# SSD decays in tiles of their own, two buffers for ec, and a HGRN norm one head earlier, in pieces

## The chip, the cores and the metric

The kernel runs on one core of one Trainium2 chip. The metric is the device time of one execution in microseconds (us). TensorE is called PE (its weight loads PEld), VectorE DVE, ScalarE ACT, GpSimd POOL and SyncE SP. Each engine works through its own queue in order; a semaphore wait holds up everything behind it on that engine.

## The reference

One inference step of two layers, each followed by a SwiGLU FFN: a Mamba-2 SSD layer and an HGRN2 layer, model width 1024, for 1024 frames of a new stream and 32 frames of a running one. The work is split in two halves of 512 and 544 columns. The scans are chunked; in the reference the SSD step is

```python
cum = jnp.cumsum(dtc * Ag, axis=1)
seg = cum[:, :, None] - cum[:, None, :]
decay = jnp.where(mask, jnp.exp(jnp.where(mask, seg, 0.0)), 0.0)
cb = jnp.einsum('btgn,bsgn->btsg', Cc, Bc)
y = jnp.einsum('btsg,btsgh,bsghp->btghp', cb, decay, xdt)
y = y + jnp.einsum('btgn,bghpn->btghp', Cc, S) * jnp.exp(cum)[..., None]
S = jnp.exp(last)[..., None, None] * S + jnp.einsum('bsgh,bsghp,bsgn->bghpn', w_end, xdt, Bc)
```

The decays of a chunk are exponentials of clamped differences of running sums; y multiplies them by C times B, and by x times dt. The HGRN layer has a gated linear recurrence per head. Each layer begins with an RMS norm: y = x * rsqrt(mean(x * x) + eps) * w.

## The kernel before, in words

Activations stand with features on the partitions and time along the row. Every large product is made of three matmuls (L314, L315, L316): the weight is split into a rounded part wh (ACT copies it, L98) and a rest wl (DVE subtracts, L101), the activation likewise (xn; h and l). A raw weight block is loaded by SP (helper `dma`, L110); three raw buffers and three pairs of wh and wl rotate. Helpers record most instructions: ACT has L98, DVE L101 (two tensors) and L104 (scalar, tensor, tensor).

The SSD layer has eight units, two halves by four groups of eight heads. A unit's work list holds the output product of the unit before (`ssd_out`), its own four z products (`ssd_z`), and late in the unit the convolutions of the next one. Its chunks of 128 columns (four in half one; four and one of 32 in half two) are spread over this list. A scheduler then places the instructions; parts marked `lifted` get a priority (`HP`, L112): a norm 600, a gate 100, a chunk 0.

A chunk (`ssd_chunk`, from L543) does this. `chunk_loads` has SP load the running sums of 2 times 4 heads, broadcast over the partitions, into two cumB tiles (tag "cb", four buffers), and the decays of the incoming state into an ec tile (tag "ec", one buffer). PE multiplies C with B (L552), DVE masks that (cbm). PE transposes x (L557), DVE makes xdt and xw from it. For each cumB tile ACT runs four Relus (each head's difference of running sums, clamped, in place), one Exp over the tile, and DVE multiplies by cbm (L570), in place too. PE transposes B (L572) and ACT copies it to Btok ("fixed<-sc 128x128"). L579 multiplies the state with C, L582 makes the new state part from Btok and xw, and L593 multiplies xdt with the decays in cumB. DVE then adds the ec part to give Y. `ssd_z` evacuates the z product on ACT (Tanh) and DVE (z<-z,mm). At the end of a unit `ssd_gate` squares Y on ACT, adds the squares on DVE, and L331 sums them over partitions for the norm (`rstd_of`, L318: squares, L331, Ln, Exp; ACT loads a table ahead of Ln and of Exp).

The HGRN layer has 16 units, two halves by eight heads (e = 0 to 7), each with chunks of which L806 to L825 are the PE part; hkv, hg, ho and hy are tiles of a head. The products of the next head (f, q, v) and the output of each two finished heads (L314 to L316 on hy) fill PE between. Half two's norm must stand before head (1, 0)'s products, which are in the work of head (0, 7). It is made with priority 600 by `norm` in the work list of head (0, 6): eight squares, the sum L331, Ln, Exp, and then for each of eight blocks of features a product on DVE (xf), a copy on ACT (h) and a subtraction on DVE (l). The results go into twelve "x" and four "cb" buffers.

Of the kernel before, what the change touches and what calls it, by code (L numbers as in the profile page):

```python
# [11 lines left out]
AF = mybir.ActivationFunctionType  # L12
# [4 lines left out]
P = 128  # L17
# [5 lines left out]
LEN = (H1, SEQ - H1 + NS)  # L23
# [14 lines left out]
C_SSDN, C_CB, C_FFN, C_HGN, C_GN, C_HG, C_LB = 0, 8, 32, 48, 56, 72, 73  # L38
# [2 lines left out]

TW = 552
FIXED = 14368
BUFS = {"x": 12, "ys": 8, "cb": 4, "xd": 2, "ec": 1, "ss": 1, "xr": 2, "n": 4, "w": 3}
WIDTH = {k: TW for k in BUFS}


@with_exitstack
def trunk_kernel(ctx, tc, x_prompt, x_sample, state_ssd, cache_conv, state_hgrn,
# [16 lines left out]
    def nm(s):  # L66
        uid[0] += 1
        return f"{s}_{uid[0]}"

    def T(tag, s, dt=F32):  # L70
        return tp.tile([P, WIDTH[tag]], dt, tag=tag, bufs=BUFS[tag], name=nm(s))

    def slot(tag, s):
        return T(tag, s, F32R) if isinstance(tag, str) else tag
# [22 lines left out]
    def act(out, in_, f, **kw):  # L97
        A.activation(out=out, in_=in_, func=f, **kw)  # L98
# [58 lines left out]
    for i in range(2):  # L157
        t = place(P)
# [8 lines left out]
    xr = place(9)  # L167
# [170 lines left out]
    XN = [xnt[:, i] for i in range(16)]  # L338
    XN2 = ["x"] * 12 + ["cb"] * 4
# [39 lines left out]
    @lifted("norm")  # L379
    def norm(h, wc, out, tags, blocks=None, r=None):  # L380

        for (b0, bn) in blocks or ((0, LEN[h]),):
            mmb = BLK[h] if blocks is None else [(0, bn)]
            if r is None:
                r = rstd_of([acc[h][m][:, b0:b0 + bn] for m in range(KD)], mmb, 1.0 / D, bn)
            for m in range(KD):
                xf = T("n", "xf")
                stt(xf[:, :bn], acc[h][m][:, b0:b0 + bn], vc[:, wc + m:wc + m + 1], r[:, :bn], MUL, MUL)
                if m == len(out):
                    out.append((slot(tags[2 * m], "h"), slot(tags[2 * m + 1], "l")))  # L390
                xh, xl = out[m]
                act(xh[:, b0:b0 + bn], xf[:, :bn], AF.Copy)
                tt(xl[:, b0:b0 + bn], xf[:, :bn], xh[:, b0:b0 + bn].bitcast(F32), SUB)
        return out
# [8 lines left out]
    st = [place(TW) for _ in range(NG)]  # L403
# [138 lines left out]
    @lifted("chunk")  # L542
    def ssd_chunk(h, g, c, S, loads, u):  # L543
        o, n, smp = CHUNKS[h][c]
        Bt, Ct, xs, Y = u["x"][0], u["x"][1], u["x"][2:], u["Y"]
        cols, elast = dts[h]
        xo = o + (3 if smp else 0)
        Bx, Cx = Bt[:, xo:xo + n], Ct[:, xo:xo + n]
        h0 = g * 8
        cums, ec = loads  # L550
        ps = psum_sc()
        PE.matmul(ps[:n, :n], Bx, Cx, start=True, stop=True)  # L552
        cbm = small("cbm")
        tt(cbm[:n, :n], ps[:n, :n], cmask[:n, :n], MUL)
        ps = psum_sc()
        for j in range(4):
            PE.transpose(ps[:n, j * P:(j + 1) * P], xs[j][:, xo:xo + n], ident)  # L557
        x3 = ps[:n, :].rearrange("p (h q) -> p h q", q=64)
        xdt, xw = T("xd", "xdt")[:, :512], T("xd", "xw")[:, :512]
        tt(xdt[:n, :].rearrange("p (h q) -> p h q", q=64), x3,  # L560
           cols[:n, c, h0:h0 + 8].unsqueeze(2).to_broadcast([n, 8, 64]), MUL)
        tt(xw[:n, :].rearrange("p (h q) -> p h q", q=64), x3,
           cols[:n, c, 64 + h0:64 + h0 + 8].unsqueeze(2).to_broadcast([n, 8, 64]), MUL)
        for q in range(2):
            cb3 = cums[q]
            for i in range(4):
                hh = 32 + h0 + 4 * q + i
                act(cb3[:n, i, :n], cb3[:n, i, :n], AF.Relu, scale=-1.0, bias=cols[:n, c, hh:hh + 1])
            act(cb3[:n, :, :n], cb3[:n, :, :n], AF.Exp, scale=-1.0)
            tt(cb3[:n, :, :n], cb3[:n, :, :n], cbm[:n, :n].unsqueeze(1).to_broadcast([n, 4, n]), MUL)  # L570
        ps = psum_sc()
        PE.transpose(ps[:n, :P], Bx, ident)  # L572
        Btok = small("Btok")
        act(Btok[:n, :], ps[:n, :P], AF.Copy)
        if ec is not None:
            y2 = psum_sc()
            y23 = y2.rearrange("p (j t) -> p j t", t=P)
            for j in range(4):
                PE.matmul(y23[:, j, :n], S[:, j * P:(j + 1) * P], Cx, start=True, stop=True)  # L579
            tt(ec[:, :, :n], y23[:, :, :n], ec[:, :, :n], MUL)  # L580
        pp = psum_sc()
        PE.matmul(pp, Btok[:n, :], xw[:n, :], start=True, stop=True)  # L582
        if ec is None:
            V.tensor_copy(S, pp)
        else:
            S3 = S.rearrange("p (h q) -> p h q", q=64)
            tt(S3, S3, elast[:, h0:h0 + 8, c:c + 1].to_broadcast([P, 8, 64]), MUL)
            tt(S, S, pp, ADD)
        y1 = psum_sc()
        y13 = y1.rearrange("p (j t) -> p j t", t=P)  # L590
        for i in range(8):
            r = 64 * (i % 2)
            PE.matmul(y13[r:r + 64, i // 2, :n], xdt[:n, i * 64:(i + 1) * 64], cums[i // 4][:n, i % 4, :n],  # L593
                      start=True, stop=True)
        yo = Y[:, :, o:o + n]
        if ec is None:
            act(yo, y13[:, :, :n], AF.Copy)
        else:
            tt(yo, y13[:, :, :n], ec[:, :, :n], ADD)
# [260 lines left out]
    def hgrn_layer(after):  # L860
        units = [(h, e) for h in range(2) for e in range(8)]
        us = [{"S": None} for _ in units]
        for f in (hgrn_f, hgrn_q, hgrn_v):
            f(0, 0, us[0])
        for i, (h, e) in enumerate(units):
            u = us[i]
            tasks = [lambda: hgrn_g(h, e, u)]
            if e % 2 == 0 and i:
                ph, pe = units[i - 1]
                tasks += [lambda m4=m4: hgrn_out(ph, pe // 2, m4, [us[i - 2]["y"], us[i - 1]["y"]])  # L870
                          for m4 in range(2)]
            if i + 1 < len(units):
                nh, ne = units[i + 1]
                tasks += [lambda f=f: f(nh, ne, us[i + 1]) for f in (hgrn_f, hgrn_q, hgrn_v)]
            if (h, e) == (0, 6):
                tasks.append(lambda: norm(1, C_HGN, xns[1], XN2))
            if (h, e) == (1, 6):
                tasks += after[:1]
            if (h, e) == (1, 7):
                tasks += after[1:]  # L880
            u["o"] = T("ys", "ho")
            if e % 2 == 0:
                yt = sp.tile([P, 4 * TW], F32R, tag="Y", bufs=1, name=nm("hy"))[:, :4 * LEN[1]]
                yp = yt.rearrange("p (j t) -> p j t", j=4)
            u["yp"] = yp
            nch = len(CHUNKS[h])
            for c in range(nch):
                second = hgrn_chunk(h, e, c, u)
                q = -(-len(tasks) // (nch - c))
                for i2, t in enumerate(tasks[:q]):  # L890
                    if i2 == HB2:
                        second()
                    t()
                if q <= HB2:
                    second()
                tasks = tasks[q:]
            hgrn_gate(h, e, u)
        return [lambda m4=m4: hgrn_out(1, 3, m4, [us[-2]["y"], us[-1]["y"]]) for m4 in range(2)]
# [6 lines left out]
    def x_stat(h, keep):  # L905

        return rstd_of([acc[h][m][:, :LEN[h]] for m in range(KD)], BLK[h], 1.0 / D, LEN[h], keep)

    def norm_pieces(h, wc, out, blocks, r):

        def piece(m, b0, bn):
            xf = T("n", "xf")
            stt(xf[:, :bn], acc[h][m][:, b0:b0 + bn], vc[:, wc + m:wc + m + 1], r[:, b0:b0 + bn], MUL, MUL)
            if m == len(out):
                out.append((XN[2 * m], XN[2 * m + 1]))
            xh, xl = out[m]
            act(xh[:, b0:b0 + bn], xf[:, :bn], AF.Copy)
            tt(xl[:, b0:b0 + bn], xf[:, :bn], xh[:, b0:b0 + bn].bitcast(F32), SUB)
        return [lambda m=m, b=b: piece(m, *b) for b in blocks for m in range(KD)]
# [209 lines left out]
    def mixed(a, b):  # L1129

        out, k = [], 0
        for i, x in enumerate(a):
            out.append(x)
            while k < len(b) and k * len(a) < (i + 1) * len(b):
                out.append(b[k])
                k += 1
        return out + b[k:]
# [98 lines left out]
    xns, dts = [[], []], [None, None]  # L1236
# [12 lines left out]
    due, r = mixer_ffn(lambda after: ssd_layer(after, w0), 0, C_FFN, True)  # L1249
# [9 lines left out]
    due, r = mixer_ffn(hgrn_layer, 1, C_FFN + 8, False)  # L1259
# [41 lines left out]
```

## Time and profile before

| | |
|---|---|
| median of three runs | 2903.72 us (2901.35 to 2903.73) |
| profiled execution, device time | 2906.18 us |
| profiled execution, span | 2904.4 us |
| mean granted clock of PE | 0.996 |
| PE busy | 2848.8 us, 98% |
| DVE busy | 2152.7 us, 74% |
| ACT busy | 1559.5 us, 54% |
| SSD layer's chunks, first to last L593 | 97.6 to 856.8 us |
| half one's first 128x512 stall of L582 in unit 1 | 187.58 us |
| the HGRN norm of half two, PE's waits | 1838 to 1846 us |

In the quoted rows a timeline gives the start, the duration, the engine, the line, the operation, output<-inputs by the program's names without buffer numbers, the shape, how many in a row, and in brackets the idle time just before with what ended it. A row of waits gives the waiting engine and line, what it waited for, the sum in us, how often, and the longest. A row of a stretch gives the start and end, its length, then the busy time (and number of instructions) of PE, PEld, DVE, ACT and POOL, then the clock that PE was granted (PEclk, 1.00 is full speed), the share of the DMA engines and GB/s.

### The profile page before, as it was taken

Reading aid. Unit: us, or ns where it says so; the run is one execution under the profiler, and the core shown is the slowest. Engines: PE = TensorE matmul, PEld = TensorE weight load, DVE = VectorE, ACT = ScalarE, POOL = GpSimd, SP = SyncE. Lnnn points to the kernel's source line nnn. Section 1 sums busy time; section 2 is a strip of 40 time slices with the busy share of each in tenths; the row PEclk is TensorE's granted clock in tenths of the full one; section 3 lists DMA queues with packets and bytes.
Section 4 is the critical chain, followed back from the end, with each engine's and each line's share of the span. In section 5 each row is a group of like instructions: output and inputs, shape, how many; then the busy total and the mean of one; then the engine's idle time right before and its main releaser. Section 6 shows DMA issues by size and latency. Waiting matters only on the chain. (4 is left out here: it accounts for less than half of the span.)

```text
span 2904.4 us, 49072 instructions
## 1 busy us (share of the span) xinstructions
PE 2848.8 (98%) x19711; PEld 2619.9 (90%) x19711; DVE 2152.7 (74%) x3744; ACT 1559.5 (54%) x2922; POOL 46.4 (2%) x156
## 2 busy tenths in 40 slices
PE   8999999999999999999999999999999999999998
PEld 7777788999988999999999888899988999999998
DVE  6777787777787977887777455655568877887777
ACT  6645645554653754456544655655554644554445
POOL 0000000000000000000000000000000000000000
PEclk9999999999999999999999999999999999999999
DMA  5443434344332333323333222222222332333223
GB/s 151 115 111 92 110 82 120 109 114 108 107 90 88 102 111 100 102 80 95 109 95 105 81 82 73 60 79 77 74 84 81 119 100 88 120 94 94 90 88 111
DMA packets 401247, 282.61 MB, mean 97 GB/s; under 512 B 22633, under 2 KB 388730, under 8 KB 401018
## 3 DMA queue, kind: packets, MB, share of 16 engines
q1 hardware_dynamic: 401018, 279.47, 33.2%
q8 instruction: 154, 2.52, 0.3%
q14 instruction: 75, 0.61, 0.1%
HBM read 271.61 MB, written 7.82 MB: 96 GB/s over the span
## 5 line engine op out<-in xcount | busy, mean ns | idle before, releaser
L98 ACT ACTIVATE wh<-raw 128x512 fp32r<-128x512 f32 (+1 forms) x688 | 557.3, 818 | 541.8 <-PE mm L315 419.5
L314 PE MATMUL mm<-xn,wh 128*128 128x272 f32 (+2 forms) x1552 | 524.8, 338 | 0.3 <-ACT wh L98 0.3
L315 PE MATMUL mm<-xn,wh 128*128 128x272 f32 (+2 forms) x1552 | 519.1, 335 | 3.8 <-issue 3.8
L316 PE MATMUL mm<-xn,wl 128*128 128x272 f32 (+2 forms) x1552 | 518.5, 334 | 3.2 <-DVE wl L101 3.2
L101 DVE TENSOR_TENSOR wl<-raw,wh 128x1024 fp32r<-128x1024 f32 x308 | 375.9, 1222 | 83.7 <-ACT wh L98 63.5
L101 DVE TENSOR_TENSOR fixed<-mm,fixed 128x272 f32<-128x272 f32 (+1 forms) x512 | 262.9, 525 | 192.7 <-PE mm L316 191.1
L314 PE MATMUL mm<-fh,wh 128*128 128x272 f32 (+1 forms) x1056 | 341.7, 325 | 1.1 <-DVE fixed L101 0.8
L315 PE MATMUL mm<-fl,wh 128*128 128x272 f32 (+1 forms) x1056 | 341.9, 324 | 0.7 <-DVE fl L101 0.7
L316 PE MATMUL mm<-fh,wl 128*128 128x272 f32 (+1 forms) x1056 | 341.7, 324 | 0.0
L316 PEld LDWEIGHTS mm<-xn,wl 128*128 128x128 f32 x1552 | 293.0, 189 | 37.3 <-issue 6.0
L314 PEld LDWEIGHTS mm<-xn,wh 128*128 128x128 f32 x1552 | 293.0, 189 | 29.5 <-issue 2.6
L315 PEld LDWEIGHTS mm<-xn,wh 128*128 128x128 f32 x1552 | 293.0, 189 | 27.1 <-issue 0.8
L101 DVE TENSOR_TENSOR wh<-raw,wh 128x512 fp32r<-128x512 f32 x380 | 257.1, 688 | 38.5 <-ACT wh L98 35.2
L989 PE MATMUL mm<-th,wh 128*128 128x272 f32 (+1 forms) x912 | 260.4, 286 | 0.1
L990 PE MATMUL mm<-tl,wh 128*128 128x272 f32 (+1 forms) x912 | 259.7, 285 | 0.0
L991 PE MATMUL mm<-th,wh 128*128 128x272 f32 (+1 forms) x912 | 259.6, 285 | 0.0
L314 PEld LDWEIGHTS mm<-fh,wh 128*128 128x128 f32 x1056 | 198.4, 188 | 17.4 <-DVE fixed L101 1.7
L315 PEld LDWEIGHTS mm<-fl,wh 128*128 128x128 f32 x1056 | 198.7, 188 | 16.3 <-DVE fl L101 1.8
L316 PEld LDWEIGHTS mm<-fh,wl 128*128 128x128 f32 x1056 | 198.7, 188 | 15.3
L989 PE MATMUL sc<-xn,wh 128*128 128x272 f32 (+1 forms) x608 | 173.2, 285 | 0.5 <-ACT wh L98 0.5
L989 PEld LDWEIGHTS mm<-th,wh 128*128 128x128 f32 x912 | 171.8, 188 | 1.9 <-ACT s L98 1.2
L990 PE MATMUL sc<-xn,wh 128*128 128x272 f32 (+1 forms) x608 | 173.2, 285 | 0.0
(251 smaller groups left out, 6637.0 us busy)
## 6 DMA issues: line engine op xcount, KB each, us to landing
raw<-in_ffn_w_down_dram SPq DMA_DIRECT2D x90, 512.0 KB, 3.5
raw<-in_ffn_w_gate_dram SPq DMA_DIRECT2D x88, 512.0 KB, 3.8
raw<-in_ffn_w_up_dram SPq DMA_DIRECT2D x88, 512.0 KB, 4.6
raw<-in_ssd_in_w_dram SPq DMA_DIRECT2D x80, 512.0 KB, 4.0
raw<-in_hgrn_in_w_dram SPq DMA_DIRECT2D x64, 512.0 KB, 4.2
cumB<-cumd SPq DMA_DIRECT2D x64, 256.0 KB, 4.5
raw<-in_ssd_out_w_dram SPq DMA_DIRECT2D x32, 512.0 KB, 3.5
raw<-in_hgrn_out_w_dram SPq DMA_DIRECT2D x16, 512.0 KB, 3.3
```

The source lines that it names most:

```text
L98: A.activation(out=out, in_=in_, func=f, **kw)
L101: (eng or V).tensor_tensor(out=out, in0=a, in1=b, op=op)
L314: PE.matmul(ps[:, :bn], a, mh, start=(k == 0), stop=False)
L315: PE.matmul(ps[:, :bn], a, ml, start=False, stop=False)
L316: PE.matmul(ps[:, :bn], b, mh, start=False, stop=(k == n - 1))
L989: PE.matmul(ps[:, :n], a, mh, start=(k == 0 and not more), stop=False, skip_group_check=True)
L990: PE.matmul(ps[:, :n], a, ml, start=False, stop=False, skip_group_check=True)
L991: PE.matmul(ps[:, :n], b, mh, start=False, stop=(k == 3), skip_group_check=True)
```

## The change

Three things. The Relus of a chunk read cumB as before but write to a new tile "dec" (tag "de", two buffers); Exp, the mask product and L593 then work on dec, so a cumB tile is read last by a Relu. The ec tile has two buffers instead of one. In the HGRN layer the statistics of half two's norm (eight squares, L331, Ln, Exp) are made by `x_stat` at the end of head (0, 5)'s work list, into a tile of their own, and the eight normalisations are separate tasks, mixed between the tasks of head (0, 6), with no priority.

```diff
-BUFS = {"x": 12, "ys": 8, "cb": 4, "xd": 2, "ec": 1, "ss": 1, "xr": 2, "n": 4, "w": 3}
+BUFS = {"x": 12, "ys": 8, "cb": 4, "xd": 2, "de": 2, "ec": 2, "ss": 1, "xr": 2, "n": 4, "w": 3}
...
         for q in range(2):
-            cb3 = cums[q]
+            cb3 = T("de", "dec")[:, :512].rearrange("p (h t) -> p h t", t=P)
             for i in range(4):
                 hh = 32 + h0 + 4 * q + i
-                act(cb3[:n, i, :n], cb3[:n, i, :n], AF.Relu, scale=-1.0, bias=cols[:n, c, hh:hh + 1])
+                act(cb3[:n, i, :n], cums[q][:n, i, :n], AF.Relu, scale=-1.0, bias=cols[:n, c, hh:hh + 1])
+            cums[q] = cb3
             act(cb3[:n, :, :n], cb3[:n, :, :n], AF.Exp, scale=-1.0)
...
+            if (h, e) == (0, 5):
+                tasks.append(lambda: r.append(x_stat(1, st[2])))
             if (h, e) == (0, 6):
-                tasks.append(lambda: norm(1, C_HGN, xns[1], XN2))
+                tasks = mixed(tasks, norm_pieces(1, C_HGN, xns[1], ((0, LEN[1]),), r[0], XN2))
...
-    def norm_pieces(h, wc, out, blocks, r):
+    def norm_pieces(h, wc, out, blocks, r, tags=XN):
...
-                out.append((XN[2 * m], XN[2 * m + 1]))
+                out.append((slot(tags[2 * m], "h"), slot(tags[2 * m + 1], "l")))
```

The number of matmuls stays. Each engine's order moves in the SSD layer and around that norm. Before, on ACT in unit 1, around chunk 2's z and Btok (z_1829 and "fixed<-sc_1888"); cumB_1857 and cumB_1859 hold chunk 3's decays, and raw_2070 is a later block of weights:

```order
L98 ACTIVATE cumB_1857<-cumB_1857,fixed 128x128 x4
L98 ACTIVATE cumB_1859<-cumB_1859,fixed 128x128
L98 ACTIVATE cumB_1857<-cumB_1857 128x512
L98 ACTIVATE z_1829<-mm_1830 128x512
L98 ACTIVATE fixed<-sc_1888 128x128
L98 ACTIVATE cumB_1859<-cumB_1859,fixed 128x128 x3
L98 ACTIVATE wh_2072<-raw_2070 128x1024
L98 ACTIVATE cumB_1859<-cumB_1859 128x512
```

The same place of the changed kernel; dec_1888 and dec_1895 hold chunk 2's decays, z_1841 and "fixed<-sc_1902" are chunk 2's too:

```order
L98 ACTIVATE dec_1888<-cumB_1779,fixed 128x128 x4
L98 ACTIVATE dec_1895<-cumB_1781,fixed 128x128
L98 ACTIVATE dec_1888<-dec_1888 128x512
L98 ACTIVATE dec_1895<-cumB_1781,fixed 128x128 x3
L98 ACTIVATE dec_1895<-dec_1895 128x512
L98 ACTIVATE wh_2088<-raw_2086 128x1024
L98 ACTIVATE z_1841<-mm_1842 128x512
L98 ACTIVATE fixed<-sc_1902 128x128
```

The decays were one chunk ahead of z and Btok and are now those of the same chunk; the weight split wh, which stood behind z and Btok, stands ahead of them.

ACT at the end of head (0, 5) before, from the squares of the head's own ho (sq_18747, rstd_18749, hy_18228) on:

```order
L98 ACTIVATE sq_18747<-ho_18531 128x512
L98 ACT_TABLE_LOAD
L98 ACTIVATE rstd_18749<-sc_18750,fixed 128x512
L98 ACTIVATE hkv_18766<-sc_18763 128x256
L98 ACT_TABLE_LOAD
L98 ACTIVATE rstd_18749<-rstd_18749 128x512
L98 ACTIVATE wh_18903<-raw_18901 128x1024
L98 ACTIVATE hy_18228<-ho_18531 128x512
```

And in the changed kernel; "fixed<-sc_18834" and the next row are the Ln of the norm's statistics, "fixed<-fixed 128x544" their Exp, sq_18849 and rstd_18851 the head's own:

```order
L98 ACT_TABLE_LOAD
L98 ACTIVATE fixed<-sc_18834,fixed 128x272
L98 ACTIVATE fixed<-sc_18837,fixed 128x272
L98 ACTIVATE ho_18603<-sc_18843 128x128
L98 ACT_TABLE_LOAD
L98 ACTIVATE fixed<-fixed 128x544
L98 ACTIVATE sq_18849<-ho_18603 128x512
L98 ACTIVATE hg_18870<-mm_18877 128x512
L98 ACTIVATE hkv_18868<-sc_18865 128x256
L98 ACT_TABLE_LOAD
L98 ACTIVATE rstd_18851<-sc_18852,fixed 128x512
```

The two table loads, the two Ln and the Exp of the norm stand ahead of the head's squares, and the head's rstd follows with two loads of its own.

PE there in the changed kernel, from the last part of head 5's output (sc_18843) to the sum of its squares (sc_18852); mm_18877 and mm_18928 are products:

```order
L826 MATMUL sc_18843<-hq_18500,fixed 128x128
L314 MATMUL mm_18877<-xn,wh_18873 128x512
L315 MATMUL mm_18877<-xn,wh_18873 128x512
L316 MATMUL mm_18877<-xn,wl_18874 128x512
L314 MATMUL mm_18877<-xn,wh_18873 128x512
L315 MATMUL mm_18877<-xn,wh_18873 128x512
L316 MATMUL mm_18877<-xn,wl_18874 128x512
L314 MATMUL mm_18928<-hy_18300,wh_18924 128x512
L315 MATMUL mm_18928<-hy_18300,wh_18924 128x512
L331 MATMUL sc_18852<-sq_18849,fixed 128x512
```

Eight products now stand between the two. Line numbers of the changed kernel are one higher here (L826 is L825 before), since its source is one line longer above.

More of the change, by code (lines that the diff above doesn't have):

```diff
@@ L862, in hgrn_layer @@
         us = [{"S": None} for _ in units]
+        r = []
         for f in (hgrn_f, hgrn_q, hgrn_v):
```

## Prediction

> **What bounds the kernel now.** I read the page's busy times first, then the table of stretches, then the groups of waits between 50 and 500 us, then the engines' timelines around single waits of TensorE.
>
> ```profile
> span 2904.4 us, 49072 instructions
> PE 2848.8 (98%) x19711; PEld 2619.9 (90%) x19711; DVE 2152.7 (74%) x3744; ACT 1559.5 (54%) x2922; POOL 46.4 (2%) x156
> ```
>
> TensorE is idle for 2904.4 - 2848.8 = 55.6 us. No matmul is removed, so an edit can win only from these 55.6 us and from stretches at a lower clock. The stretches (columns: PE, weight loads, DVE, ACT, POOL busy; PEclk; DMA) say where the idle time lies:
>
> ```profile
> 100.00:150.00 50.00, 47.05 (x261) 36.10 (x260) 44.28 (x77) 39.84 (x87) 2.95 (x8) 0.97 0.43 114
> ...
> 500.00:650.00 150.00, 150.00 (x1218) 141.40 (x1218) 116.62 (x193) 86.10 (x193) 8.19 (x32) 1.00 0.42 112
> ```
>
> The first half of the SSD layer loses 3 us in this 50; the second half loses nothing between 500 and 650. So the SSD edit can only win in half one, and can only lose in half two. What TensorE, ACT and SyncE wait for in 50 to 500 us (total, times, longest):
>
> ```profile
> ACT cumB L98 <- DMA cumB<-cumd: 49.0, 19, 8.6
> ACT wh L98 <- PE mm L315: 46.2, 18, 4.5
> ...
> PE sc L582 <- ACT wh L98: 5.0, 4, 1.7
> ...
> PE mm L316 <- DVE wl L101: 4.0, 4, 2.0
> ...
> PE sc L582 <- DVE xw L101: 3.3, 3, 1.4
> ...
> PE sc L331 <- DVE sq L101: 2.8, 2, 1.6
> ...
> PE sc L579 <- ACT fixed L98: 1.0, 1, 1.0
> ...
> PE sc L582 <- ACT fixed L98: 1.0, 1, 1.0
> ```
>
> ```profile
> SPq L110 <- PE sc L593: 51.0, 15, 5.6
> ```
>
> Eight waits of the state product L582 make 5.0 + 3.3 + 1.0 = 9.3 us. ACT's own largest wait is for the landing of cumB, and SyncE, which must issue that load, stands for 51.0 us until L593 of TensorE has read the old decays: the decays are made in place in the tile that the next load needs. One chunk of unit 1 shows how this reaches TensorE. TensorE between 187 and 199 us, then ACT and DVE from 193 us:
>
> ```profile
> 187.58 1.10 PE L582 MATMUL sc<-xw,fixed 128*128 128x512 f32 x2 [1.72 <-ACT wh L98]
> ...
> 193.46 0.38 PE L552 MATMUL sc<-ca,ca 128*128 128x128 f32 x2
> ...
> 196.51 0.39 PE L314 MATMUL mm<-xn,wh 128*128 128x512 f32 x1
> 196.74 0.39 PE L315 MATMUL mm<-xn,wh 128*128 128x512 f32 x1
> 198.29 1.10 PE L582 MATMUL sc<-xw,fixed 128*128 128x512 f32 x2 [1.16 <-ACT wh L98]
> ```
>
> ```profile
> 193.52 1.70 ACT L98 ACTIVATE cumB<-cumB,fixed 128x128 f32<-128x128 f32 x5 [5.51 <-DMA cumB<-cumd]
> 195.13 0.61 ACT L98 ACTIVATE cumB<-cumB 128x512 f32<-128x512 f32 x1
> 195.65 0.58 ACT L98 ACTIVATE z<-mm 128x512 f32<-128x512 f32 x1
> 196.13 0.27 ACT L98 ACTIVATE fixed<-sc 128x128 f32<-128x128 f32 x1
> 196.28 0.98 ACT L98 ACTIVATE cumB<-cumB,fixed 128x128 f32<-128x128 f32 x3
> 197.16 1.05 ACT L98 ACTIVATE wh<-raw 128x1024 fp32r<-128x1024 f32 x1
> ```
>
> ```profile
> 196.26 0.69 DVE L104 SCALAR_TENSOR_TENSOR z<-z,mm 128x512 f32<-128x512 f32 x1 [1.36 <-ACT z L98]
> 196.86 0.68 DVE L101 TENSOR_TENSOR xdt<-sc,fixed 128x512 f32<-128x512 f32 x1
> 197.46 0.68 DVE L101 TENSOR_TENSOR xw<-sc,fixed 128x512 f32<-128x512 f32 x1
> 198.06 0.68 DVE L101 TENSOR_TENSOR cumB<-cumB,fixed 128x512 f32<-128x512 f32 x1
> ```
>
> ACT is idle for 5.51 us until a load for the next chunk lands, then runs that chunk's Relus and Exp (193.52 to 195.65) ahead of z and Btok ("fixed<-sc") of this chunk. DVE waits for z, and xdt and xw stand behind z. xw ends at 198.14; L582, due at 197.13 (196.74 + 0.39), starts at 198.29. The label "ACT wh" is only the nearest event; the late operand is xw.
>
> **The SSD edit, part by part.** Instruction counts stay. Relus now read cumB and write "dec", so a cumB buffer is free for reloading when its last Relu has run, instead of after L593; four cumB buffers then hold loads a chunk ahead, and the 49.0 us of ACT's waits for landings can go. What takes their place is a wait of a chunk's first Relu for L593 of the chunk before, which still reads the two dec buffers. Behind that Relu on ACT are queued the next weight split wh, z and Btok.
>
> First: does the decay work fit between two L593? Five Relus take 195.13 - 193.52 = 1.61, three more 0.98, two Exps 0.52 each (195.13 to 195.65), the last mask product on DVE 0.68: 1.61 + 0.98 + 1.04 + 0.68 = 4.3 us, and with some 0.3 for two handovers 4.6. The distance in unit 1 is 198.29 - 187.58 = 10.71, by L582, which stands just ahead of L593. The shortest is in unit 0, by the starts of L593:
>
> ```profile
> 103.35 1.09 PE L593 MATMUL sc<-cumB,xdt 128*64 128x128 f32 x16
> ...
> 108.72 1.09 PE L593 MATMUL sc<-cumB,xdt 128*64 128x128 f32 x16
> ```
>
> 5.37 us, of which L593 itself takes 1.09: 4.28 us are left for 4.6. So units 1 to 3 have room, and in unit 0 the new chain can end about 0.3 us late.
>
> Second: is xw in time? In the new order ACT has wh, z, Btok behind the decays, and wh must wait until L315 has read its old buffer (the 46.2 us above), which is the product just ahead of L552. Counted from L552 at 193.46: wh 1.05, z 0.5, z on DVE 0.6, xdt 0.6, xw 0.68 = 3.43, against 197.13 - 193.46 = 3.67 until L582 is due. Margin 0.24 us. I therefore let the eight waits fall from 1.16 on average to 0.2: gain 9.3 - 1.6 = 7.7 us; bounds 0 (wh lands later) and 9.3.
>
> Third: the gate's L331 waits (2.8 us). The squares on ACT stand behind the next unit's first decays there too, and these now lack the landing wait: gain 2.5, bounds 0 and 2.8. L579's single 1.0: half. Fourth, unit 0's long wait and what came behind it:
>
> ```profile
> 128.06 0.58 PE L316 MATMUL mm<-xn,wl 128*128 128x512 f32 x1 [1.98 <-DVE wl L101]
> ```
>
> ```profile
> 128.30:131.75 3.45, 3.45 (x9) 2.03 (x9) 2.13 (x3) 3.42 (x5) 0.53 (x2) 0.51 0.45 152
> ...
> 1845.30:1852.00 6.70, 6.17 (x26) 5.92 (x27) 6.70 (x11) 2.96 (x6) 0.00 (x0) 0.50 0.27 81
> ```
>
> After a gap of 1.98 us the clock is at half for 3.45 us, which costs 1.7 more: 3.7 in all. The new order of unit 0 has ACT's decays later, beside convolution work of the next unit, so I take half, 1.85; bounds -1.2 (four chunks late by 0.3) and 3.7. The second ec buffer removes SyncE's wait for the last reader of the only one; DVE hardly waits for ec, so 0.
>
> Sum for SSD: 7.7 + 2.5 + 0.5 + 1.85 = 12.6 us; bounds -1.2 and 16.8.
>
> **The HGRN edit.** The second half's norm today stalls TensorE where it is needed. TensorE, then ACT:
>
> ```profile
> 1838.05 1.18 PE L331 MATMUL sc<-sq,fixed 128*128 128x272 f32 x4 [0.41 <-DVE sq L101]
> ...
> 1844.44 0.77 PE L314 MATMUL mm<-h,wh 128*128 128x272 f32 x4 [3.15 <-ACT h L98]
> 1845.83 0.57 PE L314 MATMUL mm<-h,wh 128*128 128x272 f32 x1 [0.62 <-DVE hg L104]
> ```
>
> ```profile
> 1837.10 1.28 ACT L98 ACT_TABLE_LOAD   x1
> ...
> 1840.93 1.28 ACT L98 ACT_TABLE_LOAD   x1
> 1842.22 0.66 ACT L98 ACTIVATE rstd<-rstd 128x544 f32<-128x544 f32 x1
> ```
>
> The two table loads and the Exp lie between the sums of squares and the first normalised tile. 0.41 + 3.15 + 0.62 = 4.18 us idle, and 6.70 us at half clock (the row 1845.30) cost 3.4: 7.6 us. With the statistics a head sooner, the tiles are ready long before their product, so these 7.6 go. But the loads, Ln and Exp are now queued on ACT at the end of head 5, ahead of that head's own squares, its rstd with two more loads, its second operand hy, and two of head 6's hkv. By the new order TensorE has eight products between the o that these squares read and their sum L331, at 0.23 each (196.51 to 196.74) some 1.9 us; ACT needs 0.27 + 1.28 + 0.66 + 0.6 = 2.8, so about 1 us of new wait. Then hkv stands behind two loads and Ln and Exp, and hy behind those and wh (1.05) and two h tiles: by the same rows some 1.1 and 2. New waits of 4.1 us, estimated; the nearest row is the present 4.18. Bounds 0 (other work covers it) and 7.6 (with the clock). Half clock once more for 3.45 us would cost 1.7; I count 1.7. Net gain 7.6 - 4.1 - 1.7 = 1.8; bounds 0 and 7.6.
>
> The last 1.7 rests on the row 128.06, where 1.98 us of idleness came just ahead of half clock. The Trainium skill, "TensorE: Matmul & The Clock Gate", section "HAM oscillation — how this bites in real kernels", says that only idle gaps above about 3.4 us do this. By that rule the new waits of 1 to 2 us would not lower the clock and the net would be 3.5. The trace disagrees (1.98 us did), so the sum above keeps the 1.7.
>
> **Total.** 12.6 + 1.8 = 14.4 us off the profiled run's 2906.18 (span 2904.4 and 1.8 around it): 2891.8. That run lies 2.46 above the median of 2903.72, so against medians I say 2890. About 0.2%, 5.8 us, is what a measurement of this kernel can tell from no change.
>
> **Rivals.** *Half of it:* z still follows a wh that waits, and the HGRN wait only moves one head up, clock included. Then SSD gives half, 6.3, HGRN 0: 2903.7 - 6.3 = 2897. For it: the margin of 0.24 us. Against it: the ACT time freed is larger.
>
> *Nothing:* L582's lateness came from z and wh, not from the landing, because wh waits for L315 whatever the decays do. 9.3 stays, the rest gives 3: 2901. For it: the label on four of the waits is wh. Against it: ACT's 5.51 us of waiting for a landing stand directly ahead.
>
> *Slower:* two dec buffers tie ACT to TensorE. If a unit's L593 come closer than the 4.6 us of the chain plus wh, z and Btok in front of it (1.05 + 0.5 + 0.15, 6.3 in all), each chunk waits. It decides when that holds outside unit 0, in half two, where nothing is lost now. Its price: waits of today's mean size, 9.3 / 8 = 1.16, in the 28 successions of 36 chunks in 8 units, 32.5 us, less the 14.4 gained: 2903.7 + 18 = 2922. Against it, the last reader of the decays by the list of cumB's instructions:
>
> ```profile
> L593 PE MATMUL sc<-cumB,xdt x576: 217/273/324, 97.6 to 856.8; 128*64 128x128 f32 x171, 32*64 32x32 f32 x21
> ```
>
> from 500 to 856.8 us there are 20 chunks, 17.8 us apart on average.
>
> *More:* HGRN's new waits are all covered and the whole 7.6 comes, SSD 14: 2903.7 - 21.6 = 2882.
>
> **Chances.** Forecast (2884 to 2895) 0.50; half of it 0.23, of which a quarter lies within 0.2%; nothing 0.13; slower 0.08; more 0.06. Faster by over 0.2% (below 2897.9): 0.50 + 0.17 + 0.06 = 0.73; within: 0.06 + 0.13 = 0.19; slower 0.08. The range runs from 2880 (nearly all bounds at their best: 16.8 + 7.6 = 24.4 off) to 2903, which leaves out the slower case and part of "nothing".
>
> **What would show it.** Right: no wait of L582 above 0.4 us in units 1 and 2; ACT's waits for cumB landings near zero; SyncE's wait for L593 gone; stretches 100 to 350 at 48.5 busy of 50 or more; half clock behind unit 0 shorter; the 3.15 us wait of the HGRN norm gone and waits of 1 to 2 us some 40 us earlier. Wrong: ACT waiting for L593 with z behind it, new waits of L593 or L582 between 500 and 857 us, or a longer stretch of half clock before 1845 than the 6.7 us now.

## The result, and the profile after

The changed kernel takes 2887.01 us (median of six runs, 2885.35 to 2888.13) where the kernel before, run beside it, takes 2902.43 us (2901.35 to 2903.73). The ratio is 0.9946 with a 95% interval of 0.9933 to 0.9959: 15.4 us, or 12 to 19 us by the interval, faster. The forecast was 2890 us, in a range of 2880 to 2903.

The page of the changed kernel's profiled run (2887.34 us):

```profile
span 2885.6 us, 49044 instructions
PE 2843.3 (99%) x19711; PEld 2618.5 (91%) x19711; DVE 2152.4 (75%) x3744; ACT 1556.9 (54%) x2922; POOL 43.5 (2%) x156
```

The idle time of TensorE is down from 55.6 to 42.3 us; the span is 18.8 us shorter. This pair of executions differs by more than the medians do (15.4 us). Three stretches of the changed kernel (PE's busy time is the first number behind the length):

```profile
100.00:150.00 50.00, 49.56 (x276) 39.07 (x275) 45.26 (x78) 37.34 (x80) 1.57 (x6) 1.00 0.44 125
200.00:250.00 50.00, 50.00 (x225) 39.64 (x224) 44.70 (x61) 29.72 (x44) 3.82 (x12) 1.00 0.36 103
500.00:650.00 150.00, 150.00 (x1222) 143.27 (x1221) 119.94 (x190) 85.16 (x182) 10.19 (x41) 1.00 0.43 112
```

100 to 150 had 47.05 us of PE and a clock of 0.97 before. Between 500 and 650 us nothing is lost, as before. The waits of ACT, TensorE and SyncE between 50 and 500 us that answer to those of before:

```profile
ACT wh L98 <- PE mm L315: 80.4, 29, 4.6
...
PE mm L316 <- DVE wl L101: 1.3, 2, 0.9
...
PE sc L583 <- DVE xw L101: 1.2, 1, 1.2
```

```profile
SPq L110 <- ACT dec L98: 32.4, 15, 3.5
```

L583 is the state product that was L582. Its eight waits of before (two in unit 0, three each in units 1 and 2) are gone; one of 1.25 us is new in unit 3, at 384.90 us, where it had none. ACT's waits for the landing of cumB, 49.0 us before, are gone from the list; ACT now waits longer (80.4 instead of 46.2 us) for L315 ahead of wh; that costs nothing by itself, because ACT has nothing else to do then. SyncE no longer waits for L593 but for the Relus (ACT dec). One chunk of unit 1 (L594, the y product, was L593), TensorE, then ACT, then DVE:

```profile
187.29 0.38 PE L552 MATMUL sc<-ca,ca 128*128 128x128 f32 x2
...
190.81 1.03 PE L583 MATMUL sc<-xw,fixed 128*128 128x512 f32 x2
191.77 1.09 PE L594 MATMUL sc<-dec,xdt 128*64 128x128 f32 x16
```

```profile
187.26 1.06 ACT L98 ACTIVATE wh<-raw 128x1024 fp32r<-128x1024 f32 x1 [3.05 <-PE mm L315]
188.23 0.58 ACT L98 ACTIVATE z<-mm 128x512 f32<-128x512 f32 x1
188.70 0.27 ACT L98 ACTIVATE fixed<-sc 128x128 f32<-128x128 f32 x1
188.86 1.57 ACT L98 ACTIVATE dec<-cumB,fixed 128x128 f32<-128x128 f32 x5
```

```profile
188.72 0.69 DVE L101 TENSOR_TENSOR xdt<-sc,fixed 128x512 f32<-128x512 f32 x1
189.32 0.68 DVE L104 SCALAR_TENSOR_TENSOR z<-z,mm 128x512 f32<-128x512 f32 x1
189.91 0.69 DVE L101 TENSOR_TENSOR xw<-sc,fixed 128x512 f32<-128x512 f32 x1
```

ACT is done with the chunk's decays early and idles 3.05 us; wh, z and Btok follow in the order forecast; xw ends at 190.60, and L583, ahead of which TensorE is not idle, starts at 190.81. The margin is 0.2 us. The next chunk's Relus (dec, 188.86) start with no wait, before L594 (191.77) has read this chunk's decays; no row of this kernel's list has a Relu waiting for L594. The two dec buffers thus limit how far ahead the scheduler places the decays, but they are not two fixed places: in the built program tiles of this width share their places, and two successive chunks have their decays at different addresses.

The HGRN norm, TensorE's waits and ACT's work around the second of them:

```profile
1786.09 1.13 PE L331 MATMUL sc<-sq,fixed 128*128 128x512 f32 x2 [1.01 <-ACT sq L98]
1792.51 0.49 PE L822 MATMUL sc<-hkv 128*128 128x128 f32 x2 [0.74 <-ACT hkv L98]
1794.71 0.33 PE L811 MATMUL sc<-fixed,hk 128*128 128x128 f32 x1 [1.04 <-ACT ho L98]
1825.27 1.12 PE L331 MATMUL sc<-sq,fixed 128*128 128x512 f32 x2 [0.88 <-ACT sq L98]
```

```profile
1788.09 1.28 ACT L98 ACT_TABLE_LOAD   x1
1789.39 0.69 ACT L98 ACTIVATE rstd<-sc,fixed 128x512 f32<-128x512 f32 x1
1789.97 0.27 ACT L98 ACTIVATE ho<-sc 128x128 f32<-128x128 f32 x1
1790.26 1.28 ACT L98 ACT_TABLE_LOAD   x1
1791.56 0.63 ACT L98 ACTIVATE rstd<-rstd 128x512 f32<-128x512 f32 x1
1792.09 0.36 ACT L98 ACTIVATE hkv<-sc 128x256 f32<-128x256 f32 x1
```

3.67 us of waits in place of 4.18. The first comes some 36 us of the program earlier than the first of before (1838.05 less 1786.09, less the 16.3 us that the SSD layer has gained by then), the last a head later, at 1825. hkv, for which L822 waits, stands behind the two table loads of the head's own norm.

### The profile page after: what moved, and what is told of

It is laid out like the page before. It is cut to its first block, busy times and chain, and to the rows that moved or that the text cites. A ratio compares the mean times of both kernels' runs of the same rounds, so it can differ in the third digit from the quotient of the medians.

```text
span 2885.6 us, 49044 instructions
## 1 busy us (share of the span) xinstructions
PE 2843.3 (99%) x19711; PEld 2618.5 (91%) x19711; DVE 2152.4 (75%) x3744; ACT 1556.9 (54%) x2922; POOL 43.5 (2%) x156
## 4 chain that ended last, share of the span: by engine, by line
PE 92%; DVE 5%; ACT 1%; issue 1%; DMA 1%; SPq 0%; POOL 0%; DVEq 0%; ACTq 0%
PE mm L314 19%; PE mm L315 19%; PE mm L316 19%; PE mm L995 5%; PE mm L993 5%; PE mm L994 5%; PE sc L995 4%; PE sc L993 4%; PE sc L994 4%; PE sc L594 1%; PE sc L583 1%; PE sc L331 1%; PE sc L580 1%; DVE fixed L101 1%; PE sc L822 1%
## 5 line engine op out<-in xcount | busy, mean ns | idle before, releaser
L315 PE MATMUL mm<-xn,wh 128*128 128x272 f32 (+2 forms) x1552 | 519.3, 335 | 5.2 <-issue 5.2
L315 PE MATMUL mm<-fl,wh 128*128 128x272 f32 (+1 forms) x1056 | 341.9, 324 | 0.8 <-DVE fl L101 0.8
L315 PEld LDWEIGHTS mm<-xn,wh 128*128 128x128 f32 x1552 | 293.2, 189 | 27.6 <-issue 1.2
L315 PEld LDWEIGHTS mm<-fl,wh 128*128 128x128 f32 x1056 | 198.7, 188 | 16.4 <-DVE fl L101 1.8
```

The source lines that it names most:

```text
L315: PE.matmul(ps[:, :bn], a, ml, start=False, stop=False)
```

## The experiments

Each kernel is compared with the kernel before on the same chip; its median changed from one set of runs to the next (2902.4, 2900.5, 2901.5, 2901.2 and 2899.9 us), so ratios are compared across sets, not medians. The theory: half one's waits come from a cumB load that lands late while ACT, in order, stands at the Relu with z and Btok behind it; freeing the tile at the Relu starts the load early enough. Rivals: it is the order of the decays (own chunk instead of one ahead), the second ec buffer, more buffer space, or the HGRN move.

### The two halves of the change, each alone

The SSD edits alone keep the old norm:

```diff
-            if (h, e) == (0, 5):
-                tasks.append(lambda: r.append(x_stat(1, st[2])))
             if (h, e) == (0, 6):
-                tasks = mixed(tasks, norm_pieces(1, C_HGN, xns[1], ((0, LEN[1]),), r[0], XN2))
+                tasks.append(lambda: norm(1, C_HGN, xns[1], XN2))
```

> The SSD edits alone (dec tiles, two ec buffers); the norm of the HGRN layer's second half stays as before. The changed kernel took 15.4 us off (2902.4 to 2887.0). Theory: the eight waits of L582 and the two of L331 in half one were made by cumB loads that landed late, and their going is 12 to 14 us: 2888.5 to 2890.5, with the 3.15 us wait of the HGRN norm and the half clock behind it still there. Rival that the HGRN move brought half of it: 2894 to 2896. Rival that it brought nothing: 2887.

Measured: 2887.93 us beside 2900.5, ratio 0.9952 (0.9940 to 0.9965): 12.6 us. Its profile keeps the old wait of the HGRN norm and the half clock behind it:

```profile
1827.42 1.96 PE L314 MATMUL mm<-h,wh 128*128 128x272 f32 x5 [3.14 <-ACT h L98]
```

```profile
1826.80:1833.60 6.80, 6.06 (x24) 5.49 (x25) 6.80 (x10) 3.74 (x6) 0.00 (x0) 0.50 0.23 77
```

The HGRN move alone, on the SSD code of before (parts of the edit; the Relus write to cumB again):

```diff
-            cb3 = T("de", "dec")[:, :512].rearrange("p (h t) -> p h t", t=P)
+            cb3 = cums[q]
...
-            cums[q] = cb3
...
-"de": 2, "ec": 2,
+"ec": 1,
```

> The HGRN move alone; the SSD layer as before. Theory: 4.2 us idle and 3.4 us of half clock go, waits of 3.7 us come a head earlier, in sum 2 to 4 us: 2898.5 to 2900.5. Rival that it only shifts the stall: 2902.4. Rival that the new waits are covered: 2895.

Measured: 2899.72 us beside 2900.5, ratio 0.9996 (0.9987 to 1.0005): 0.8 us, not to be told from nothing. Its profile has the new waits (1.01, 0.75, 1.05 and 0.85 us) and, behind the third, a stretch at half clock:

```profile
1810.50:1813.90 3.40, 3.35 (x8) 2.70 (x9) 1.94 (x5) 0.82 (x3) 0.00 (x0) 0.50 0.12 26
```

So the SSD edits carry the gain; what the HGRN move brings is between a loss of 1.5 and a gain of 3.8 us by its interval.

### One ec buffer

```diff
-"de": 2, "ec": 2,
+"de": 2, "ec": 1,
```

> The changed kernel with one ec buffer instead of two. Theory: the second buffer hides nothing that TensorE waits for: 2886 to 2888.5. Rival: SyncE, held at the ec load until the last reader is done, holds up the weight loads behind it: 2890 or more, with waits of L314 or L316 for wl in units 1 to 3.

Measured: 2887.66 us, ratio 0.9953 (0.9941 to 0.9966). The second ec buffer brings nothing that shows in the time. Its trace shows two things that the changed kernel's does not. First, Relus do wait here for L594 of the chunk before, as the prediction had it, and the time is the same within the intervals:

```profile
ACT dec L98 <- PE sc L594: 42.1, 14, 4.5
```

Second, unit 0's long wait of TensorE is back:

```profile
124.42 0.50 PE L316 MATMUL mm<-xn,wl 128*128 128x512 f32 x1 [2.09 <-DVE wl L101]
```

All five kernels here with one ec buffer have this wait (1.64 to 2.35 us); none of the nine profiles with two has it. So it follows the ec buffer, and the 2 us are of the size of the difference of the ratios (0.9953 and 0.9946), which the intervals cannot tell from nothing. How the buffer reaches that wait is not traced.

### Six cumB buffers and no new tile

The kernel before, with one number changed:

```diff
-"cb": 4,
+"cb": 6,
```

> Before, with six cumB buffers instead of four and nothing else: the decays are still made in place and a chunk ahead, there is no wait for dec buffers, and the space taken is that of the two dec tiles. Theory (what counts is that the load lands in time): most of the SSD gain without any new tile, 2889 to 2893, and ACT's waits for cumB landings under 10 us. Rival (what counts is that the decays are made in their own chunk, behind which z and Btok follow at once): at most 3 us, 2899 to 2903, with L582's waits in units 1 and 2 still near 1.2 us each.

Measured: 2906.26 us, ratio 1.0019 (1.0010 to 1.0028): slower. The time expected of the theory was not reached. But the landing waits, which it expected to go, did not go either. ACT's and TensorE's waits of this kernel from 50 to 500 us, then SyncE's:

```profile
ACT cumB L98 <- DMA cumB<-cumd: 36.0, 17, 5.2
...
PE sc L582 <- DVE xw L101: 5.2, 5, 1.2
```

```profile
SPq L110 <- PE sc L593: 47.8, 14, 5.1
```

The order on ACT says why: chunk 3's decays (cumB_1857) now stand ahead of chunk 1's z (z_1741), where the kernel before had chunk 2's there (buffer numbers are shown here):

```
L98 ACTIVATE cumB_1857<-cumB_1857,fixed 128x128 x4
L98 ACTIVATE cumB_1859<-cumB_1859,fixed 128x128
L98 ACTIVATE cumB_1857<-cumB_1857 128x512
L98 ACTIVATE z_1741<-mm_1742 128x512
```

The scheduler spent the buffers on running the decays one chunk further ahead, not on loading ahead of them, so ACT waits for landings as before. This left both the theory and the order rival standing.

### Four dec buffers

The changed kernel, with which the decays can run a chunk ahead again (and with one ec buffer, which costs nothing that showed in the time above):

```diff
-"de": 2, "ec": 2,
+"de": 4, "ec": 1,
```

> The changed kernel with four dec buffers (and one ec buffer): cumB tiles are still freed by the Relus, but with four buffers the decays can again be made a chunk ahead, as their order on ACT shows. First theory (only the early landing of cumB counts): as the changed kernel, 2886 to 2889. New theory after the run with six cumB buffers (what counts is that two buffers hold the decays back to their own chunk, so that z and Btok are not queued behind the next chunk's decays): ACT waits for landings again, L582 waits of about 1 us come back in units 1 and 2, and 2895 to 2902. Between 2889 and 2895 both have a share.

Measured: 2889.64 us, ratio 0.9959 (0.9946 to 0.9971). On ACT the decays of chunk 2 stand ahead of chunk 1's z again. Between 50 and 500 us no Relu waits for a landing (two waits of wh, 0.9 us in sum, are put down to one), and the state product has no wait in units 0 to 2:

```profile
ACT dec L98 <- PE sc L594: 21.6, 7, 4.5
...
PE sc L583 <- DVE xw L101: 1.2, 1, 1.2
```

The expectation gave both theories a share between 2889 and 2895 us, and the time lies just inside. By the ratios this kernel may be some 4 us above the changed one, but the intervals overlap, and about 2 us of it can be unit 0's wait, which it has too (1.64 us). What the order rival asked for, landing waits and L582's waits of about 1 us in units 1 and 2, is not there. So the order a chunk ahead does little harm where no Relu waits for a landing: the order rival falls as the main cause, and the theory stands in this form: what counts is that a Relu doesn't wait for a landing, and the buffer that the Relu frees brings that about, while a longer ring of tiles that L593 frees does not. A Relu's wait for L594 (21.6 us here, 42.1 with one ec buffer) does no harm that shows.

### Two cumB buffers

Two dec and two cumB buffers, together the four of before (the second ec buffer stays, one tile more than before); two of the tiles of the HGRN layer's normalised input become dec buffers:

```diff
-"cb": 4,
+"cb": 2,
...
-    XN2 = ["x"] * 12 + ["cb"] * 4
+    XN2 = ["x"] * 12 + ["cb"] * 2 + ["de"] * 2
```

> The changed kernel with two cumB buffers instead of four, so cumB and dec together take the four buffers that cumB took before (two of the tiles that held the normalised activations of the HGRN layer's second half move from cumB to dec buffers). Theory: a load now starts when a chunk's Relus are done, some 2 us after the preceding L593, and has until the next chunk's Relus, 9.3 us later in units 1 and 2, to land; the landing takes 4.5 us, so it is in time there: within 3 us of the changed kernel, 2886 to 2890, ACT's waits for landings under 10 us, some of them in unit 0. Rival: it is the four extra us of lead from two more buffers that helps: 2895 to 2902, landing waits near the 49.0 us of before.

Measured: 2884.26 us, ratio 0.9941 (0.9928 to 0.9953). ACT's waits for landings between 50 and 500 us:

```profile
ACT dec L98 <- DMA cumB<-cumd: 7.7, 8, 2.4
```

That is below the range expected, on the good side; by the ratios it is not to be told from the changed kernel. The gain needs no more tiles for the decays: a load that starts at the Relu has most of a chunk to land. That more cumB buffers or a longer lead bring the gain is refuted.

### Where the new wait begins to cost

Every Relu issued twice, then one dec buffer:

```diff
                 act(cb3[:n, i, :n], cums[q][:n, i, :n], AF.Relu, scale=-1.0, bias=cols[:n, c, hh:hh + 1])
+                act(cb3[:n, i, :n], cums[q][:n, i, :n], AF.Relu, scale=-1.0, bias=cols[:n, c, hh:hh + 1])
```

> The changed kernel with each of the 288 Relus issued twice, with the same result: 2.4 us more on ACT per chunk in the chain behind the preceding L593. It tells where the dec buffers' wait begins to cost. Theory: the chain of 4.6 becomes 7.0 us, the distance between chunks is 9.3 in units 1 and 2 and more in half two, and ACT idles some 3 us ahead of each wh; only unit 0, with 5 to 6 us, is late, by some 1.6 us in three chunks: 2890 to 2895. Rival: the chain has no room, each of 28 chunk successions is late by 2 us: 2930 or more.

Measured: 2894.85 us, ratio 0.9978 (0.9968 to 0.9987): by the ratios about 9 us above the changed kernel. (The execution that was profiled, 2890.78 us, is the fastest of ten, so its trace shows only part of that.) The first four chunks of unit 0 begin their y products at 93.5, 101.2, 109.2 and 116.6 us (97.5, 103.2, 108.5 and 114.4 in the changed kernel): some 2 us more between them, filled with other products. Units 1 and 2 keep their distance of 9.3. As in the changed kernel no Relu waits for the y product. In half two, two waits are new:

```profile
545.27 0.39 PE L314 MATMUL mm<-xn,wh 128*128 128x272 f32 x1 [1.79 <-ACT pre L98]
```

```profile
653.04 0.39 PE L314 MATMUL mm<-xn,wh 128*128 128x272 f32 x1 [2.11 <-ACT pre L98]
```

With one dec buffer (`"de": 1`):

> The changed kernel with one dec buffer (two ec): a chunk's second four heads can be decayed only when the first four products of L593 are done, so in each chunk TensorE's second half of L593 stands behind four Relus, an Exp and a mask product. Theory: this is the price of the wait that the change adds where nothing hides it, 1.3 + 0.5 + 0.7 = 2.5 us and handovers, some 3 us in 36 chunks, less what TensorE can do in between: 40 to 110 us above the changed kernel, 2930 to 3000. Rival: the scheduler fills it with products, under 10 us.

Measured: 2903.08 us, ratio 1.0003 (0.9994 to 1.0012). That is 16 us above the changed kernel, under the theory's range and over the rival's. Part of it is in the y products themselves; the groups of L594 between 90 and 860 us, of this kernel and of the changed one:

```profile
L594 PE MATMUL sc<-dec,xdt 128*64 128x128 f32 (+1 forms) x568 | 45.9, 279 | 2.3 <-ACT xn L98 2.3
```

```profile
L594 PE MATMUL sc<-dec,xdt 128*64 128x128 f32 (+1 forms) x576 | 38.7, 273 | 0.0
```

The scheduler splits each chunk's y products in two and puts other products between: two runs of 0.66 us where one took 1.09, in sum 7.2 us. The last y product begins 22.1 us later than in the changed kernel (862.6 and 840.5). Beside the 7.2 there are three waits that the changed kernel does not have, the first of 4.09 us, the others of 2.28 (the row above) and 1.06 us near 815, and half clock behind them: 6.8 us after the first, 3.4 after the others, which cost 5.1.

```profile
428.88 0.59 PE L316 MATMUL mm<-xn,wl 128*128 128x272 f32 x1 [4.09 <-DVE wl L101]
```

```profile
428.00:434.80 6.80, 5.92 (x26) 5.93 (x27) 6.70 (x8) 3.43 (x6) 2.12 (x4) 0.50 0.85 214
```

```profile
817.00:820.40 3.40, 3.40 (x15) 2.69 (x13) 3.08 (x6) 2.42 (x8) 0.00 (x0) 0.50 0.55 117
```

No Relu of this kernel waits for L594 between 50 and 870 us. So the 16 us come with the order that the scheduler makes for one buffer; what a Relu's wait costs where nothing hides it is not shown by this run.

### The HGRN move, better placed

The statistics in the middle of head 5's tasks:

```diff
-                tasks.append(lambda: r.append(x_stat(1, st[2])))
+                tasks.insert(2, lambda: r.append(x_stat(1, st[2])))
```

> The changed kernel with the norm's statistics in the middle of head 5's tasks instead of at their end, so that its two table loads, Ln and Exp are over before the head's own squares and rstd. Theory: the new waits of 1.01, 0.74, 1.04 and 0.88 us come from those loads in a row, and most go: 2.5 to 3.7 us below the changed kernel, 2883.5 to 2885 where that is 2887. Rival: they come from somewhere else (the eight h copies, hkv): within 1 us of the changed kernel, with the waits in place.

Measured: 2886.18 us, ratio 0.9948 (0.9935 to 0.9960); the waits have other places and about the same sum. The larger ones:

```profile
1786.66 0.49 PE L822 MATMUL sc<-hkv 128*128 128x128 f32 x2 [1.00 <-ACT hkv L98]
1792.94 0.49 PE L822 MATMUL sc<-hkv 128*128 128x128 f32 x2 [0.71 <-ACT hkv L98]
...
1795.86 0.49 PE L822 MATMUL sc<-hkv 128*128 128x128 f32 x2 [1.38 <-DVE fixed L809]
...
1826.85 1.13 PE L331 MATMUL sc<-sq,fixed 128*128 128x512 f32 x2 [0.53 <-ACT sq L98]
```

3.62 us, and 0.45 in two smaller ones, beside 3.67. The theory that the end of the list was the wrong place fell. Next, the loads taken away instead of moved: only the squares in mid-list, L331, Ln and Exp next to head 5's own, so that two table loads fall away (101 on ACT where the changed kernel has 103).

```diff
-    def rstd_of(tiles, blocks, scale, width, keep=None):
+    def rstd_of(tiles, blocks, scale, width, keep=None, second=None):
...
+        if second:
+            r2, tot2 = second
+            for (b0, bn) in BLK[1]:
+                ps = psum_sc()
+                PE.matmul(ps[:, :bn], ones, tot2[:, b0:b0 + bn], start=True, stop=True)
+                act(r2[:, b0:b0 + bn], ps[:, :bn], AF.Ln, bias=epsc[:, 0:1], scale=1.0 / D)
         act(r[:, :width], r[:, :width], AF.Exp, scale=-0.5)
+        if second:
+            act(r2[:, :LEN[1]], r2[:, :LEN[1]], AF.Exp, scale=-0.5)
```

> The changed kernel, with the squares of the HGRN norm made in the middle of head 5's tasks, and its L331, Ln and Exp made next to those of head 5's own norm, Ln by Ln and Exp by Exp, so that the two table loads of the statistics fall away (2 times 1.28 us on ACT). Theory: what TensorE waits for there is ACT's time in loads, Ln and Exp ahead of hkv and hy; of the 3.7 us some 2 go: 2884.5 to 2886 where the changed kernel is at 2887. Rival: the chain of chunks through ACT and DVE sets those waits by itself: 2887, waits as in the changed kernel.

Measured: 2882.36 us, ratio 0.9937 (0.9923 to 0.9950). TensorE's waits there fall to 2.04 us:

```profile
1771.27 0.33 PE L819 MATMUL sc<-fixed,hk 128*128 128x128 f32 x1 [1.60 <-DVE fixed L817]
```

```profile
1818.14 0.49 PE L815 MATMUL sc<-hq,hk 128*128 128x128 f32 x2 [0.44 <-DVE hq L104]
```

None of them is ACT's any more. The time is below the range expected. To see whether two cumB buffers and the pairing beat the changed kernel, both edits together and the changed kernel again, on one chip:

> Two cumB buffers and the paired statistics together. Theory: two cumB buffers are neither better nor worse than four, and the pairing is worth 2 to 4 us: 2882 to 2884.5 beside 2901.5 of before. If the 2.7 us by which two cumB buffers came out below the changed kernel were real and add up: 2879.5 to 2881.

Measured: 2882.80 us beside 2899.9, ratio 0.9942 (0.9929 to 0.9956).

> The changed kernel again, on the same chip as the combination: 2885.5 to 2888 beside 2901.5 of before. If it comes out at 2883 to 2884.5, the differences to the two last variants were of the chip or of chance and not of the kernels.

Measured: 2883.65 us, ratio 0.9945 (0.9932 to 0.9957), in the range that the expectation gave to chip or chance. The combination is 0.85 us below it, and the intervals lie over each other. Pairing took 1.6 us of waits off in the trace; that it shortens the kernel is not shown. Nor is it shown that two cumB buffers are better than four: the 2.7 us between the medians are less than the 3.4 by which the changed kernel's own median moved.

## Why the prediction was right, point by point

**What bounds it.** Right: the gain came from TensorE's idle time in half one, and half two lost little, a wait of 1.34 us at 800. The signs named for "right" came, but that the new HGRN waits are 0.74 to 1.04 us and not 1 to 2.

**Eight waits of L582, gain 7.7 of 9.3.** Measured 9.3 - 1.2 = 8.1. All eight went to zero where 0.2 each was kept; the new one in unit 3 was not foreseen. That the two nearly cancel is luck. DVE took xdt ahead of z, which the sum had behind it. The margin of 0.24 us is 0.2 in the trace; both of its terms, 3.43 and 3.67, came out some 0.1 shorter (3.31 and 3.52).

**The decay chain.** Right that units 1 to 3 have room, but the wait from which the chain was counted, a Relu's for L593, is not in the changed kernel (188.86 before 191.77 above). With one ec buffer it is there and harmless. In unit 0 the forecast 0.3 us of lateness is not seen: the distances are 5.7, 5.4 and 5.8 us (97.5 to 114.4). Doubling the Relus lengthens them by some 2 us, which fits that ACT's decay work sets the pace there.

**L331, gain 2.5 of 2.8; L579, half of 1.0.** L331's rows are absent in units 1 and 2; one new wait of 0.44 us stands at 125 us. Measured 2.4. L579's wait for ACT went; L580, the same product, has one of 0.48 for DVE at 388.49, beside the new one of L583. The size is as forecast, the wait another.

**Unit 0's wait and its half clock, gain 1.85 of 3.7.** The changed kernel has neither, the whole 3.7. This is the term of the SSD sum that was mis-sized, and its reason was not the one given: the prediction laid it to the later decays and put the second ec buffer at 0, but in all the profiles the wait goes with the second ec buffer (2.09 us with one). The half clock behind it came in two of the five profiles that have the wait, so that 1.7 us of it are of the execution.

**SSD sum, 12.6.** The SSD edits alone measured 12.6 against medians. In the two profiled runs the last y product begins 16.3 us sooner:

```profile
L594 PE MATMUL sc<-dec,xdt x576: 217/273/324, 97.5 to 840.5; 128*64 128x128 f32 x171, 32*64 32x32 f32 x21
```

840.5 against 856.8. The terms above come to 8.1 + 2.4 + 0.5 + 3.7 = 14.7 us, less a new wait of 1.34 us at 800; some 3 us of this pair remain. About 1.9 of them can lie at the edges of the gaps, an estimate: in the rows 196.51 and 196.74 of before products follow each other at 0.23 us and last 0.39, so a gap costs 0.16 more than the idle time shown, and TensorE's lists from 50 to 900 us have 20 waits before and 8 after. So the match of 12.6 with 12.6 is partly luck: in the traces single terms are larger, and the new wait, which was not forecast, takes some back.

**HGRN, gain 7.6 - 4.1 - 1.7 = 1.8.** The old waits went and new ones of 3.67 came: L331 1.01 where about 1 was forecast, hkv 0.74 for 1.1. The 2 us forecast for hy did not come; L811 waits 1.04 for ho instead, behind the same wh and h tiles, and the 0.88 us at 1825 was not forecast. Half clock behind them came in the move alone (the row 1810.50, behind 1.05 us) and not in the changed kernel, so counting 1.7 was right in one execution of the two. The Trainium skill's rule that the prediction set aside ("TensorE: Matmul & The Clock Gate", section "HAM oscillation — how this bites in real kernels") would have given none. The move alone measured 0.8 us, within an interval that holds 1.8 and zero: this term is not confirmed.

**The rivals.** "Half of it" fell, since z behind a wh that waits is in time. "Nothing" fell with the landing waits. "Slower" was not seen: with two dec buffers Relus that wait for L594 cost nothing that shows (one ec buffer), and the 16 us that one dec buffer gives back came with the order and not with such a wait. "More" (2882) was not reached by the changed kernel.

## What to carry to other kernels

When an in-order engine waits for a load whose buffer a late reader holds, copy out with the first operation that reads it, so that this operation frees the buffer: two such buffers did what six longer-held ones did not. Before adding buffers, look in the order at what the scheduler will run further ahead with them. A number of buffers is first a limit on the scheduler: whether an engine waits for the buffer has to be read in the trace. A step moved to where an engine seems free takes its table loads along, and the waits move with them; pairing it with the same functions took ACT's away in the trace.

## What the runs showed of the hardware

Half clock came behind short gaps, and not each time. In the second FFN TensorE waits 1.26 us at the same matmul in every kernel. The changed kernel:

```profile
2532.40 0.39 PE L995 MATMUL mm<-xn,wh 128*128 128x272 f32 x1 [1.26 <-DVE wh L101]
```

```profile
2533.20:2536.60 3.40, 3.40 (x17) 3.40 (x16) 3.00 (x5) 1.03 (x2) 0.00 (x0) 0.50 0.00 0
```

The kernel before:

```profile
2553.11 0.39 PE L991 MATMUL mm<-xn,wh 128*128 128x272 f32 x1 [1.25 <-DVE wh L101]
```

```profile
2552.00:2558.00 6.00, 4.89 (x38) 4.89 (x39) 5.70 (x12) 2.81 (x7) 0.00 (x0) 1.00 0.01 3
```

The first is followed by 3.4 us at half clock, 1.7 us lost, the second by none. Longer waits did it each time: in all four profiles with a wait above 3 us (3.14 with the SSD edits alone, 3.15 before and with six cumB buffers, 4.09 with one dec buffer) 6.7 to 6.8 us at half clock stood behind it. Such a difference is as large as several of the terms argued about here, and can be part of why single executions differ by more than an edit of 1 or 2 us.
